# A diffusion block with a gated recurrence on one core: a recurrence with fewer arrays, its gates on quarters of the array, squares moved between engines

## The chip, the cores and the metric

The kernel runs on one core of a Trainium2 chip. The core has a matrix engine (TensorE, PE in the profile), a vector engine (VectorE, DVE), an engine for activation functions (ScalarE, ACT), a general engine (GpSimd, POOL) and a queue engine that issues most transfers (SyncE, SP). The metric is the device time of one execution in microseconds, as the median of several runs.

## The reference, cut to what matters

A token of the 2048 x 1024 input is normalised and modulated, projected to 1536 columns, mixed over time in three branches, projected back, and passed through a convolutional FFN. The change touches the branch with the gated recurrence, and small parts of the others:

```python
r = sigmoid(block_diag(xh, w_a) + b_a)          # 8 heads of 64 x 64, two directions
i = sigmoid(block_diag(xh, w_x) + b_x)
log_a = -8 * r * softplus(-lam)
a = exp(log_a)
bterm = sqrt(-expm1(2 * log_a)) * (i * xf)
h[t] = a[t] * h[t-1] + bterm[t]                 # forward, and backward from the other end
...
ya = gelu(z[..., 512:1024]) * (h_f + h_b)       # gates
yb = pool_group(...)                            # window means of width 2, 4, 8, 16
yc = gmlp_group(...)                            # gelu, norm, 128 x 128 mixing over tokens
mix = concat([ya, yb, yc]) @ w_out
```

The context of 256 tokens runs through the same recurrence first, and its last states start those of the 2048 tokens.

## The kernel before, in words

Activations lie with channels on the 128 partitions and tokens along the row, in four chunks of 512 tokens (`CH`). Weights and activations are split into a high and a low fp16 part, and each product is three matmuls (`mm3`, L356), so that a block of 128 output channels by 512 tokens is 24 matmuls of 512 columns. The mixer fills the first 553 us. It is written as a list of steps (`ORDER`, L37): `x` loads and normalises a chunk, `c` runs the recurrence of the context, `a` projects and convolves a chunk of the recurrent branch, `f` and `b` are a chunk's forward and backward recurrence, `g` is half a step of gMLP, `p` a chunk of pooling, `G` the gates, `m` the modulation vectors, `w` the preparation of the output weights. `P` and `Q` are channel tiles 0, 1 and 2, 3. The list gives priorities; a scheduler places the instructions from it, and each engine then runs its own queue in order, with semaphores between the engines.

A unit of the recurrence is one channel tile and one direction in one chunk; two go together (a pair, `lru_units`, L506). `coeffs` (L440) multiplies the block-diagonal 128 x 128 gate matrices `gwt` in fp32 into two PSUM banks, `rp` and `ip`, and takes two sigmoids and a tanh on ACT. `coeffs2` takes exp on ACT, then r x r and i x xa on POOL and (r x r + 1) x tanh on DVE (`combine`, L459). `coeffs3` takes the square root on ACT and the product i x root on POOL; then DVE scans over time (`scan`, L475). A unit has a buffer of four arrays r, i, t, q of 512 columns, and there are two buffers (`lru_tile`, L176). The forward result goes to DRAM (`hfd`); the backward one is added to it (`join`, L520). Functions of ACT come in table sets, and `act` (L133) keeps instructions of one set together; sigmoid and tanh, exp, the root, and gelu are four sets, each with a table load.

Squares with a sum along the row, from which scales are computed, are taken on ACT (`sumsq`, L149) or on DVE (`vsumsq`, L152): on DVE those of the gated product (`gates`, L640), of the pooling result (`pool_br`, L539) and of the output weights (`wout_stats`, L684). After the mixer, `fold` (L284) joins the FFN's modulation with its gains; `project` then multiplies tokens by the output weights, and the FFN follows.

Of the kernel before, what the change touches and what calls it, by code (L numbers as in the profile page):

```python
# [41 lines left out]
m6 w2 b0P G1Q m6 w2 b0Q G0P m9 G0Q w9 w9  # L42
# [26 lines left out]
def block_kernel(ctx: ExitStack, tc: tile.TileContext, x, xT, ctx_d, ctxT, cc, crow, cols_d, wm01, bm01, wmT,  # L69
# [127 lines left out]
    brow = lru_tile([2, 2048], F32, "brow")  # L197
    lx = load_x(0)
    r23 = lru_tile([128, 2, 1024], F32, "r23")
# [22 lines left out]
    def stats_first(xt):  # L222
        acc = early.tile([128, CH], F32, tag="acc", name="acc")
# [164 lines left out]
    def lam_consts():  # L388
# [21 lines left out]
        V.tensor_scalar(klam, p, -8.0, None, op0=OP.mult)  # L410

# [27 lines left out]

    def coeffs(j, d, xa, w, c=None, bank=None):  # L440
# [12 lines left out]
    def coeffs2(cs, xas, w):  # L453
        for c in cs:
            act(c[0][:, :w], c[0][:, :w], AF.Exp, scale=c[4])
        for c, xa in zip(cs, xas):
            combine(c, xa, w)

    def combine(c, xa, w):  # L459
        r, i, t, q, k = c  # L460
        G.tensor_tensor(q[:, :w], r[:, :w], r[:, :w], op=OP.mult)
        G.tensor_tensor(i[:, :w], i[:, :w], xa, op=OP.mult)
        V.scalar_tensor_tensor(t[:, :w], q[:, :w], 1.0, t[:, :w], op0=OP.add, op1=OP.mult)

    def coeffs3(cs, w):
        for c in cs:
            act(c[2][:, :w], c[2][:, :w], AF.Sqrt, scale=-1.0)
        for c in cs:
            finish_b(c, w)

    def finish_b(c, w):
        i, t = c[1], c[2]
        G.tensor_tensor(i[:, :w], i[:, :w], t[:, :w], op=OP.mult)

    def scan(o, c, w, init, rev):  # L475
        r, i = c[0][:, :w], c[1][:, :w]
# [15 lines left out]
    def lru_ctx(js):  # L492
        jd = [(j, d) for j in js for d in range(2)]
        ts = [lru_tile([128, 4, CH], F32, "lrc") for j in js]
        cs = [coeffs(j, d, xac[0][:, j, :], LC, ts[j - js[0]][:, :, d * LC:(d + 1) * LC]) for j, d in jd]
        coeffs2(cs, [xac[0][:, j, :] for j, d in jd], LC)
        coeffs3(cs, LC)
        for (j, d), c in zip(jd, cs):
            q = c[3]
# [6 lines left out]
    def lru_units(d, n, js, sink):  # L506
        cs = [coeffs(j, d, Y[n][:, j, :], CH, bank=b) for j, b in zip(js, (pB, pA))]
        coeffs2(cs, [Y[n][:, j, :] for j in js], CH)
        coeffs3(cs, CH)
        for j, c in zip(js, cs):  # L510
            o = c[3]
# [86 lines left out]
    def gmlp():  # L598
        ws = wslot["uv"]
        for tp in range(8):  # L600
# [33 lines left out]
            yc = mix.tile([128, 2, 256], F32, tag="yc", bufs=1, name="yc")  # L634
            A.activation(yc, tp_ps.rearrange("p (c t) -> p c t", c=2), AF.Identity)
            sumsq(guv[0].rearrange("p (c t) -> p c t", c=2), yc, ysq[:, n, 6 + r:7 + r])
# [3 lines left out]
    def gates(n, js):  # L640
        for j in js:
            if True:
                ps = pA(f"gt{j}")
                mm_in(ps, 4 + j, n * CH, CH)
                g = late.tile([128, CH], F32, tag="gg", bufs=3, name="gg")
# [588 lines left out]
```

## Time and profile before

| | |
|---|---|
| median of three runs | 2155.48 us (2154.54 to 2159.58) |
| the profiled execution | 2155.6 us, span 2153.8 us |
| PE busy | 2022.0 us, 94% of the span |
| DVE busy | 1593.2 us, 74% |
| ACT busy | 1194.6 us, 55% |
| POOL busy | 610.1 us, 28% |
| mean granted clock of PE | 0.972 |

The table says how busy each engine is over everything. It does not say which engine is last in a stage. For that, the rows further down cut the span into stretches: 148 to 345 us is the forward recurrence beside convolution and gMLP, 345 to 553 us the backward recurrence beside pooling and gates, and from 553 us the output projection starts; the FFN runs at an even pace from about 860 to 2060 us.

### The profile page before, as it was taken

The page shows a single profiled execution, that of the slowest core. Times are in us where ns is not written, and L with a number is a line of the kernel's source. Part 1 is how long each engine was busy: PE and PEld are TensorE (multiplying, and loading weights), DVE is VectorE, ACT ScalarE, POOL GpSimd, SP SyncE. Part 2 cuts the span into 40 slices and gives each one's busy share as a digit, 9 for nine tenths or more (in the row PEclk, how much of TensorE's full clock was granted, in tenths as well). Part 3 has the DMA queues.
Part 4 walks back from the last instruction along what each step waited for, and adds up shares of the span by engine and source line. Part 5 has one row for each costly group of instructions (what it writes and reads, how often), then busy time and mean ns, then how long its engine had stood idle before and what let it go on. Part 6 is the DMA issues. An engine that isn't in the chain of part 4 may idle for free.

```text
span 2153.8 us, 24277 instructions
## 1 busy us (share of the span) xinstructions
PE 2022.0 (94%) x9215; PEld 933.4 (43%) x9215; DVE 1593.2 (74%) x2214; ACT 1194.6 (55%) x1665; POOL 610.1 (28%) x457
## 2 busy tenths in 40 slices
PE   6878989788899998999999999999999999999995
PEld 1433444333455443444444444444444444444442
DVE  5687788999655359978667776867777686777876
ACT  4676756455254555656565554655556465555453
POOL 1233334445155510101121121212112121221156
PEclk8889999998999999999999999999999999999998
DMA  7521152512433210315455454544545454454248
GB/s 297 183 88 74 69 166 89 180 35 85 135 136 114 79 64 20 130 66 132 89 117 98 79 124 72 108 78 102 94 88 100 74 103 88 100 95 69 40 157 156
DMA packets 73480, 224.78 MB, mean 104 GB/s; under 512 B 7442, under 2 KB 18066, under 8 KB 68498
## 3 DMA queue, kind: packets, MB, share of 16 engines
q0 software_dynamic: 21312, 77.60, 21.4%
q1 hardware_dynamic: 52052, 145.64, 19.6%
q8 instruction: 72, 1.18, 0.2%
q14 instruction: 44, 0.36, 0.1%
HBM read 120.45 MB, written 102.76 MB: 104 GB/s over the span
## 4 chain that ended last, share of the span: by engine, by line
PE 55%; DVE 3%; POOL 1%; DMA 1%; ACT 1%; issue 1%; POOLq 0%; SPq 0%; DVEq 0%; ACTq 0%
PE up L359 12%; PE up L360 12%; PE up L361 12%; PE dn L1054 6%; PE dn L1056 6%; PE dn L1055 6%; DVE cv L1011 2%; DMA hT<-accd 1%; POOL hT L1069 0%; DVE hT L1086 0%; DVE hT L1060 0%; DMA wm<-in_wmT_dram 0%; POOL fms L159 0%; PE sct L121 0%; POOL out_dram L1087 0%
## 5 line engine op out<-in xcount | busy, mean ns | idle before, releaser
L1011 DVE SCALAR_TENSOR_TENSOR cv<-z,cols,cv 128x1008 f32<-128x1008 f32 (+3 forms) x704 | 870.4, 1250 | 276.6 <-ACT cv L1005 188.7
L359 PE MATMUL up<-hT,uw 128*128 128x512 f16 x1408 | 534.1, 379 | 2.6 <-ACT z L846 2.6
L361 PE MATMUL up<-hT,uw 128*128 128x512 f16 x1408 | 534.1, 379 | 0.0
L360 PE MATMUL up<-hT,uw 128*128 128x512 f16 x1408 | 534.1, 379 | 0.0
L1071 POOL DMA_DIRECT2D accd<-dd x132 | 114.2, 865 | 704.1 <-ACT dd L1065 697.9
L846 ACT ACTIVATE z<-up,upinv 128x512 f32<-128x512 f32 x176 | 120.5, 685 | 311.2 <-PE up L361 310.8
L1065 ACT ACTIVATE dd<-dn,gdi 128x512 f32<-128x512 f32 x320 | 214.2, 680 | 115.0 <-PE dn L1056 107.5
L1054 PE MATMUL dn<-dw,gs 128*128 128x512 f16 x704 | 267.2, 380 | 7.1 <-ACT dd L1065 5.3
L1055 PE MATMUL dn<-dw,gs 128*128 128x512 f16 x704 | 267.5, 380 | 0.0
L1056 PE MATMUL dn<-dw,gs 128*128 128x512 f16 x704 | 265.8, 380 | 0.0
L360 PEld LDWEIGHTS <-uw 128*128 128x128 f16 x1408 | 137.8, 98 | 167.5 <-issue 3.6
L359 PEld LDWEIGHTS <-uw 128*128 128x128 f16 x1408 | 139.0, 99 | 164.7 <-issue 0.6
L361 PEld LDWEIGHTS <-uw 128*128 128x128 f16 x1408 | 137.8, 98 | 166.5 <-issue 0.6
L832 POOL TENSOR_TENSOR uw<-ur,uw 128x2048 f16<-128x2048 f32 x22 | 89.5, 4070 | 168.9 <-ACT ur L831 168.9
L135 ACT ACT_TABLE_LOAD x77 | 98.8, 1283 | 47.4 <-PE rp L443 28.8
L1005 ACT ACTIVATE cv<-z,cols 128x1024 f32<-128x1024 f32 x88 | 106.0, 1206 | 2.0
L1055 PEld LDWEIGHTS <-gs 128*128 128x128 f16 x704 | 68.8, 98 | 86.8 <-issue 9.5
L1054 PEld LDWEIGHTS <-gs 128*128 128x128 f16 x704 | 72.2, 103 | 78.8 <-issue 0.8
L1056 PEld LDWEIGHTS <-gs 128*128 128x128 f16 x704 | 68.9, 98 | 83.5 <-issue 0.6
L986 POOL TENSOR_TENSOR dw<-dr,dw 128x1024 f16<-128x1024 f32 x22 | 46.4, 2127 | 141.8 <-PE dn L1056 100.3
L150 ACT ACTIVATE junk<-g 128x1024 bf16<-128x1024 f32 x44 | 46.3, 1053 | 59.9 <-DVE g L1019 59.9
L878 PE MATMUL wo<-wo,ysp 128*128 128x512 f16 x256 | 77.1, 383 | 1.0 <-ACT gm L807 1.0
(302 smaller groups left out, 3076.7 us busy)
## 6 DMA issues: line engine op xcount, KB each, us to landing
accd<-dd POOLq DMA_DIRECT2D x132, 512.0 KB, 5.1
ur<-in_wup_dram SPq DMA_DIRECT2D x22, 1024.0 KB, 5.6
wm<-in_wmT_dram SPq DMA_DIRECT2D x64, 256.0 KB, 2.9
dr<-in_wdn_dram SPq DMA_DIRECT2D x22, 512.0 KB, 4.6
hT<-in_wm_dram SPq DMA_DIRECT2D x8, 1024.0 KB, 14.4
xt<-in_xT_dram SPq DMA_DIRECT2D x8, 1024.0 KB, 7.1
ro<-in_wout_dram SPq DMA_DIRECT2D x16, 512.0 KB, 3.8
xr<-in_x_dram SPq DMA_DIRECT2D x16, 512.0 KB, 3.6
```

What stands on the lines that cost most here:

```text
L135: ins = A.activation(out_, in_, func, **kw).ins
L359: T.matmul(ps, wh(k), hh(k), start=(k == 0), stop=False)
L360: T.matmul(ps, wh(k), hl(k), start=False, stop=False)
L361: T.matmul(ps, wl(k), hh(k), start=False, stop=(k == KT - 1))
L846: A.activation(z[:, ab, b * 8:(b + 1) * 8, :], ps.rearrange("p (r x) -> p r x", x=64), AF.Identity, scale=upinv[:, c:c + 1])
L1005: A.activation(t, z[:, ab, r0:r0 + 16, :].rearrange("p r x -> p (r x)"), AF.Identity, bias=col("fcb", c + NP * ab), scale=wt(0, 0))
L1011: V.scalar_tensor_tensor(o, z[:, ab, ya + dy:yb + dy, xa + dx:xb + dx], wt(dy, dx), o, op0=OP.mult, op1=OP.add)
L1054: T.matmul(ps[h], hi, wh, start=i == 0, stop=False)
L1055: T.matmul(ps[h], hi, wl, start=False, stop=False)
L1056: T.matmul(ps[h], lo, wh, start=False, stop=i == n - 1)
L1065: A.activation(d[:, h * CH:(h + 1) * CH], ps[h], AF.Copy, scale=di)
L1071: G.dma_start(accd[t], d, accum_op=OP.add)
```

## The change

- The root: with t = tanh(log a / 2), 1 - a^2 is -t (1 + a)^2, where before it was -tanh(log a)(1 + a^2). The tanh takes half the factor (a new column of constants, -4 softplus, in the place of `lam`), the root is taken of -t directly, and (1 + a) is multiplied into i x xa. POOL's r x r and the array q go; the scan writes into t.
- A unit has three arrays, and there are four buffers instead of two, in a pool of their own. A pool `lru0` holds what shared those buffers in the first 90 us.
- The gates are 64 x 64 matmuls on quarters of the array: for each half of the channels one for `rp` and one for `ip`. The result of `ip` lands with its halves exchanged, and its sigmoid is two instructions of 64 partitions. `gwt` is loaded without its zero blocks, by eight loads.
- The squares in `gates`, `pool_br` and `wout_stats` are taken on ACT.
- `yc` lies in the gMLP's own tile, `acc` in a tile of the squares, and there are two `gg` buffers instead of three.
- `fold` of the FFN is a step of the list (`F`) ahead of the last two backward pairs.

```diff
-m6 w2 b0P G1Q m6 w2 b0Q G0P m9 G0Q w9 w9
+w2 F b0P G1Q w2 b0Q G0P G0Q w9 w9
...
-    gwt = mix.tile([128, 4, 4, 128], F32, name="gwt")
-
-    def lru_tile(shape, dt, name):
-        return mix.tile(shape, dt, tag="lru", bufs=2, name=name)
+    gwt = mix.tile([128, 4, 4, 64], F32, name="gwt")
+    HALVES = (slice(0, 64), slice(64, 128))
...
+        V.tensor_scalar(lam, p, -4.0, None, op0=OP.mult)
...
-        T.matmul(rp[:, :w], gwt[:, j, 2 * d, :], xa, start=True, stop=True)
-        T.matmul(ip[:, :w], gwt[:, j, 2 * d + 1, :], xa, start=True, stop=True)
-        c = lru_tile([128, 4, CH], F32, "lru") if c is None else c
-        r, i, t, q = (c[:, a, :] for a in range(4))
-        act(r[:, :w], rp[:, :w], AF.Sigmoid, bias=col("ba", 4 * d + j))
-        act(i[:, :w], ip[:, :w], AF.Sigmoid, bias=col("bx", 4 * d + j))
-        k = klam[:, 4 * d + j:4 * d + j + 1]
-        act(t[:, :w], r[:, :w], AF.Tanh, scale=k)
-        return r, i, t, q, k
...
+        for h, o in zip(HALVES, HALVES[::-1]):
+            T.matmul(rp[h, :w], gwt[h, j, 2 * d, :], xa[h], start=True, stop=True)
+            T.matmul(ip[o, :w], gwt[h, j, 2 * d + 1, :], xa[h], start=True, stop=True)
+        c = lru_tile("lru") if c is None else c
+        r, i, t = (c[:, a, :w] for a in range(3))
+        act(r, rp[:, :w], AF.Sigmoid, bias=col("ba", 4 * d + j))
+        for h, o in zip(HALVES, HALVES[::-1]):
+            act(i[h], ip[o, :w], AF.Sigmoid, bias=col("bx", 4 * d + j)[h])
+        act(t, r, AF.Tanh, scale=col("lam", 4 * d + j))
+        return r, i, t, klam[:, 4 * d + j:4 * d + j + 1]
+
+    def coeffs2(cs, xas):
+        for r, i, t, k in cs:
+            act(r, r, AF.Exp, scale=k)
+        for r, i, t, k in cs:
+            act(t, t, AF.Sqrt, scale=-1.0)
+        for (r, i, t, k), xa in zip(cs, xas):
+            G.tensor_tensor(i, i, xa, op=OP.mult)
+            V.scalar_tensor_tensor(i, r, 1.0, i, op0=OP.add, op1=OP.mult)
+            G.tensor_tensor(i, i, t, op=OP.mult)
...
-                    vsumsq(a[:, 0:CH], yb[n - 1], ysq[:, n - 1, 4 + pt:5 + pt])
+                    sumsq(a[:, 0:CH], yb[n - 1], ysq[:, n - 1, 4 + pt:5 + pt])
...
-                vsumsq(g, Y[n][:, j, :], ysq[:, n, j:j + 1])
+                sumsq(g, Y[n][:, j, :], ysq[:, n, j:j + 1])
...
-            vsumsq(r, r, t[:, k:k + 1])
+            sumsq(r, r, t[:, k:k + 1])
...
-    S.dma_start(gwt, gw.rearrange("j p g c -> p j g c"))
+    for j in range(4):
+        for h in HALVES:
+            S.dma_start(gwt[h, j], gw[j, h, :, h])
...
+    lruc = tc.tile_pool(name="lru", bufs=4, side="right")
```

The order of instructions shows three places. The first is PE, where the gates of a forward pair of chunk 1 follow a gMLP block (`rp` and `ip` are the two gate banks, `Y1_94` is the chunk's convolved input, `uv` a block of the gMLP; the numbers tell buffers and allocations apart); before:

```order
L361 MATMUL uv_1520<-wsu3_666,hT_82 128x512
L443 MATMUL rp_1556<-Y1_94,gwt_101 128x512
L444 MATMUL ip_1557<-Y1_94,gwt_101 128x512
L443 MATMUL rp_1564<-Y1_94,gwt_101 128x512
L444 MATMUL ip_1565<-Y1_94,gwt_101 128x512
```

and after, the same pair:

```order
L451 MATMUL rp_1597<-Y1_94,gwt_101 64x512
L452 MATMUL ip_1598<-Y1_94,gwt_101 64x512
L451 MATMUL rp_1597<-Y1_94,gwt_101 64x512
L452 MATMUL ip_1598<-Y1_94,gwt_101 64x512
L451 MATMUL rp_1608<-Y1_94,gwt_101 64x512
L452 MATMUL ip_1609<-Y1_94,gwt_101 64x512
L451 MATMUL rp_1608<-Y1_94,gwt_101 64x512
L452 MATMUL ip_1609<-Y1_94,gwt_101 64x512
```

Four matmuls of 128 rows have become eight of 64, and `rp` and `ip` still take turns. The second place is ACT in the backward stretch, one pair with the gates after it (`gt` is the gate projection in PSUM, `gg` its gelu, `klam` and `cols` constants); before:

```order
L135 ACT_TABLE_LOAD
L135 ACTIVATE lru<-rp,cols 128x512
L135 ACTIVATE lru<-lru,klam 128x512
L135 ACTIVATE lru<-ip,cols 128x512
L135 ACTIVATE lru<-rp,cols 128x512
L135 ACTIVATE lru<-ip,cols 128x512
L135 ACTIVATE lru<-lru,klam 128x512
L135 ACT_TABLE_LOAD
L135 ACTIVATE lru<-lru,klam 128x512 x2
L135 ACT_TABLE_LOAD
L135 ACTIVATE lru<-lru 128x512 x2
L135 ACT_TABLE_LOAD
```

and after, from the second tanh of a pair on (`ysq` collects the sums of squares, `yb` is a chunk of the pooling result):

```order
L135 ACTIVATE lru<-ip,cols 64x512 x2
L135 ACTIVATE lru<-lru,cols 128x512
L135 ACT_TABLE_LOAD
L135 ACTIVATE lru<-lru,klam 128x512 x2
L135 ACT_TABLE_LOAD
L135 ACTIVATE lru<-lru 128x512 x2
L135 ACT_TABLE_LOAD
L135 ACTIVATE gg<-gt_3192,inv 128x512
L150 ACTIVATE gg,ysq<-Y_92 128x512
L135 ACTIVATE gg<-gt_3221,inv 128x512
L150 ACTIVATE gg,ysq<-Y_92 128x512
L150 ACTIVATE pa,ysq<-yb 128x512
```

The sets and their loads stay as they were; the sigmoids of `ip` have doubled, and three squares stand behind the gelus. The third place is POOL in the same stretch, two backward pairs of chunk 2 (`hf` is the forward result read back); before:

```order
L462 TENSOR_TENSOR lru_2739<-lru_2739,Y23_92 128x512
L462 TENSOR_TENSOR lru_2747<-lru_2747,Y23_92 128x512
L461 TENSOR_TENSOR lru_2739<-lru_2739 128x512
L461 TENSOR_TENSOR lru_2747<-lru_2747 128x512
L473 TENSOR_TENSOR lru_2739<-lru_2739 128x512
L473 TENSOR_TENSOR lru_2747<-lru_2747 128x512
L523 TENSOR_TENSOR Y23_92<-lru_2739,hf_2765 128x512
L523 TENSOR_TENSOR Y23_92<-lru_2747,hf_2770 128x512
L462 TENSOR_TENSOR lru_2921<-lru_2921,Y23_92 128x512
```

and after:

```order
L467 TENSOR_TENSOR lru_2800<-lru_2800,Y23_92 128x512
L467 TENSOR_TENSOR lru_2811<-lru_2811,Y23_92 128x512
L469 TENSOR_TENSOR lru_2800<-lru_2800 128x512
L469 TENSOR_TENSOR lru_2811<-lru_2811 128x512
L517 TENSOR_TENSOR Y23_92<-lru_2800,hf_2828 128x512
L517 TENSOR_TENSOR Y23_92<-lru_2811,hf_2833 128x512
L467 TENSOR_TENSOR lru_2986<-lru_2986,Y23_92 128x512
```

Two of eight instructions of a pair are gone; the next pair's first product still stands behind the sum with the forward result.

## Rows read from the trace of the kernel before

**Rows 1.** Windows: stretch, length, busy us (instructions) of each engine, granted clock, DMA share, GB/s.

```profile
148.00:345.00 197.00, 177.44 (x745) 82.17 (x745) 154.58 (x318) 137.79 (x188) 71.44 (x64) 0.96 0.26 89
345.00:553.00 208.00, 169.99 (x667) 75.98 (x665) 195.43 (x330) 100.04 (x129) 91.25 (x62) 0.91 0.33 104
...
860.00:2060.00 1200.00, 1196.01 (x5600) 549.62 (x5599) 900.47 (x950) 677.36 (x844) 229.07 (x170) 1.00 0.46 94
```

**Rows 2.** Waits, 345 to 553 us, ACT then PE: us in total, times, longest.

```profile
ACT lru L135 <- DVE lru L463: 31.7, 11, 7.0
ACT L135 <- PE rp L443: 27.8, 4, 9.3
ACT gg L135 <- PE gt L361: 17.6, 6, 4.5
ACT L135 <- DVE state L514: 12.7, 2, 10.2
...
PE pp L535 <- DVE pb L574: 23.1, 6, 6.6
PE sct L121 <- DVE gsfmm L297: 4.6, 1, 4.6
```

**Rows 3.** Waits, 148 to 345 us, DVE.

```profile
DVE lru L463 <- POOL lru L461: 22.7, 5, 7.3
```

**Rows 4.** DVE, lines 479 and 153: count, ns min/median/max, first and last start.

```profile
L479 DVE TENSOR_TENSOR_SCAN lru<-lru,state x32: 1251/1274/2287, 163.8 to 535.6; 128x512 f32<-128x512 f32 x32
...
L153 DVE SCALAR_TENSOR_TENSOR gg<-Y x16: 659/679/1793, 399.0 to 551.0; 128x512 f32<-128x512 f32 x16
L153 DVE DVE_READ_ACCUMULATOR gg<-Y x16: 75/76/84, 399.6 to 551.7; 128x1 f32 x16
L153 DVE SCALAR_TENSOR_TENSOR ro<-ro x8: 1194/1664/2297, 374.8 to 406.8; 128x1024 f32<-128x1024 f32 x8
```

**Rows 5.** Line 153 in a window; line 479 by form (busy us, mean ns), 345 to 553.

```profile
345.00:553.00 208.00, 35.79 (x64) 0.91 0.33 104
...
L479 DVE TENSOR_TENSOR_SCAN lru<-lru,state 128x512 f32<-128x512 f32 x16 | 26.4, 1650 | 2.0 <-POOL lru L473 2.0
```

**Rows 6.** Timeline, DVE then POOL: start us, us, engine, line, operation.

```profile
463.44 0.69 DVE L562 TENSOR_TENSOR pa<-pb 128x521 f32<-128x521 f32 x1
...
464.75 1.66 DVE L562 TENSOR_TENSOR pb<-pa 64x513 f32<-64x513 f32 x1
...
464.32 3.22 POOL L473 TENSOR_TENSOR lru<-lru 128x512 f32<-128x512 f32 x2 [1.35 <-ACT lru L135]
```

**Rows 7.** ACT's squares by form, 148 to 345 us: count, busy us, mean ns, idle.

```profile
L150 ACT ACTIVATE ws<-rw 128x1024 bf16<-128x1024 f32 x6 | 6.3, 1052 | 5.5 <-DMA rw<-in_win_dram 5.5
L150 ACT ACTIVATE guv<-yc 128x512 f32<-128x512 f32 x5 | 3.1, 627 | 0.1
...
L150 ACT ACTIVATION_READ_ACCUMULATOR guv<-yc 128x1 f32 x5 | 0.9, 186 | 0.0
```

**Rows 8.** POOL's r x r by form, 345 to 553 us.

```profile
L461 POOL TENSOR_TENSOR lru<-lru 128x512 f32<-128x512 f32 x16 | 19.7, 1248 | 5.8 <-ACT lru L135 5.8
```

**Rows 9.** Timeline of ACT: two sigmoids of a pair.

```profile
456.38 0.67 ACT L135 ACTIVATE lru<-ip,cols 128x512 f32<-128x512 f32 x1
456.95 0.68 ACT L135 ACTIVATE lru<-rp,cols 128x512 f32<-128x512 f32 x1
```

**Rows 10.** Timeline of PE: the gates of a pair between fp16 blocks.

```profile
474.05 0.38 PE L360 MATMUL pl<-hT,ws 128*128 128x512 f16 x1
474.26 0.38 PE L361 MATMUL pl<-hT,ws 128*128 128x512 f16 x1
474.48 1.02 PE L443 MATMUL rp<-Y,gwt 128*128 128x512 f32 x2
...
477.91 0.38 PE L359 MATMUL gt<-hT,ws 128*128 128x512 f16 x1
```

**Rows 11.** Timeline of SP's queue: the load of the gate matrices.

```profile
22.67 0.39 SPq L718 DMA_DIRECT2D gwt<-in_gw_dram  x1
```

More of the change, by code (lines that the diff above doesn't have):

```diff
@@ L173, in block_kernel @@
     mix = mixc.__enter__()
-    gwt = mix.tile([128, 4, 4, 128], F32, name="gwt")
-    def lru_tile(shape, dt, name):
-        return mix.tile(shape, dt, tag="lru", bufs=2, name=name)
+    gwt = mix.tile([128, 4, 4, 64], F32, name="gwt")
+    HALVES = (slice(0, 64), slice(64, 128))
+    lru0c = tc.tile_pool(name="lru0", bufs=1, side="right")
+    lru0 = lru0c.__enter__()
     earlyc = tc.tile_pool(name="early", bufs=1)
@@ L196, in block_kernel @@
     wmv = hT.bitcast(F32).rearrange("p a k t -> p (a k t)").rearrange("p (k t) -> p k t", k=KT)
-    brow = lru_tile([2, 2048], F32, "brow")
+    brow = lru0.tile([2, 2048], F32, name="brow")
     lx = load_x(0)
-    r23 = lru_tile([128, 2, 1024], F32, "r23")
+    r23 = lru0.tile([128, 2, 1024], F32, name="r23")
     win_raw = [rawt(f"rw{j}") if j < 2 else r23[:, j - 2, :] for j in range(4)]
@@ L222, in stats_first @@
     def stats_first(xt):
-        acc = early.tile([128, CH], F32, tag="acc", name="acc")
+        acc = early.tile([128, 2, CH], F32, tag="xs", bufs=2, name="acc")[:, 0, :]
         sq = early.tile([128, 2, CH], F32, tag="xs", bufs=2, name="sq")
@@ L438, in block_kernel, with lru_tile @@
     state = const.tile([128, 4, 2], F32, name="state")
+    def lru_tile(name):
+        return lrup.tile([128, 3, CH], F32, tag="lru", name=name)
     def coeffs(j, d, xa, w, c=None, bank=None):
@@ L450, in coeffs @@
-        act(t[:, :w], r[:, :w], AF.Tanh, scale=k)
-        return r, i, t, q, k
[L453 to L463, printed above, removed]
@@ L493, in lru_ctx @@
         jd = [(j, d) for j in js for d in range(2)]
-        ts = [lru_tile([128, 4, CH], F32, "lrc") for j in js]
+        ts = [lru_tile("lrc") for j in js]
         cs = [coeffs(j, d, xac[0][:, j, :], LC, ts[j - js[0]][:, :, d * LC:(d + 1) * LC]) for j, d in jd]
-        coeffs2(cs, [xac[0][:, j, :] for j, d in jd], LC)
-        coeffs3(cs, LC)
+        coeffs2(cs, [xac[0][:, j, :] for j, d in jd])
         for (j, d), c in zip(jd, cs):
-            q = c[3]
+            q = c[2]
             scan(q, c, LC, 0.0, d == 1)
@@ L507, in lru_units @@
         cs = [coeffs(j, d, Y[n][:, j, :], CH, bank=b) for j, b in zip(js, (pB, pA))]
-        coeffs2(cs, [Y[n][:, j, :] for j in js], CH)
-        coeffs3(cs, CH)
+        coeffs2(cs, [Y[n][:, j, :] for j in js])
         for j, c in zip(js, cs):
-            o = c[3]
+            o = c[2]
             scan(o, c, CH, state[:, j, d:d + 1], d == 1)
@@ L633, in gmlp @@
                                 v[:, ct * 128:(ct + 1) * 128], ident)
-            yc = mix.tile([128, 2, 256], F32, tag="yc", bufs=1, name="yc")
+            yc = guvt[:, :, 0:256]
             A.activation(yc, tp_ps.rearrange("p (c t) -> p c t", c=2), AF.Identity)
-            sumsq(guv[0].rearrange("p (c t) -> p c t", c=2), yc, ysq[:, n, 6 + r:7 + r])
+            sumsq(guvt[:, :, 256:512], yc, ysq[:, n, 6 + r:7 + r])
             S.dma_start(ybc[n][:, 2:4, r * 256:(r + 1) * 256], yc)
@@ L644, in gates @@
                 mm_in(ps, 4 + j, n * CH, CH)
-                g = late.tile([128, CH], F32, tag="gg", bufs=3, name="gg")
+                g = late.tile([128, CH], F32, tag="gg", bufs=2, name="gg")
                 act(g, ps, AF.Gelu_apprx_tanh, scale=inv[:, 4 + j:5 + j])
                 V.tensor_tensor(Y[n][:, j, :], g, Y[n][:, j, :], op=OP.mult)
-                vsumsq(g, Y[n][:, j, :], ysq[:, n, j:j + 1])
+                sumsq(g, Y[n][:, j, :], ysq[:, n, j:j + 1])
     mcol = const.tile([128, 2, 32], F32, name="mcol")
@@ L753, in late_open, with fold_ffn @@
         S.dma_start(pwt, pw)
-    late = latec = pwt = None
+    late = latec = pwt = gs_f = sc_f = None
+    def fold_ffn():
+        nonlocal gs_f, sc_f
+        gs_f, sc_f, _ = fold("gsf", col("gpf", 0, 8), mcol[:, 0, 8:16], mcol[:, 0, 16:24])
     def prep_ins(*js):
@@ L837, in block_kernel @@
     gm2 = row_of("gm2", on_, 0, col("gqm", 0, 8))
-    gs_f, sc_f, _ = fold("gsf", col("gpf", 0, 8), mcol[:, 0, 8:16], mcol[:, 0, 16:24])
     def up(c, z, w, order=(0, 1, 2, 3)):
```

16 lines of the change are left out of this document (6 added, 10 removed).

## The prediction

> **What bounds the kernel now.** I read the busy time by stage first, because the share over the whole span hides that the stages have different limits [rows 1]. From the first projection at 553 us on, TensorE (PE) is all but full; in the FFN it is busy for 1196.0 of 1200 us. The order of instructions on every engine behind the first projection is the same in both kernels (one small VectorE pair apart), so that nothing before 553 us can shorten what follows it; a microsecond won in the mixer moves the end by a microsecond. The change therefore lives in 553 us, and there the limits differ. In 345 to 553 us, where the backward recurrence, the gates and the pooling branch run, VectorE (DVE) is busy for 195.4 of 208 us, PE for 170.0, ScalarE (ACT) for 100.0 [rows 1]. The waits of that stretch agree: PE waits 23.1 us in front of the pooling matmul for DVE, ACT waits 31.7 us at the root for DVE's product, 27.8 us for `rp` and 12.7 us for a recurrence buffer that DVE still reads [rows 2]. DVE is last. In 148 to 345 us (forward recurrence, convolution, gMLP) PE leads with 177.4 of 197 us and DVE follows with 154.6; DVE idles there for 22.7 us at the combine, waiting for GpSimd's (POOL) square [rows 1, 3].
>
> A second reading matters for the sum. DVE's times contain waits for POOL: a scan is 1.27 us by its median and up to 2.29, a square of `gg` 0.68 and up to 1.79 [rows 4]. The timeline shows why: the 64x513 add takes 1.66 us while POOL runs its product from 464.32, although the larger 128x521 add just before took 0.69 [rows 6]. An instruction of POOL thus costs DVE time as well.
>
> **The change, part by part.** The sum is made against the profiled execution, 2155.6 us (span 2153.8 and 1.8 around it); the median of the runs shown is 2155.48, so nothing has to be corrected.
>
> *Squares to ACT.* 32 squares with their accumulator reads leave DVE, 35.8 us of its busy time in the backward stretch [rows 5]. Not all of it is work: at the shortest durations it is 24 squares of 512 at 0.66 (those of `yb` have the shape of those of `gg`), 8 of 1024 at 1.19 and 32 reads at 0.08, or 28 us; the other 8 us are waits for POOL, and will fall on the neighbouring instruction [rows 4]. ACT pays 24 squares at 0.63 + 0.19 and 8 long ones at 1.05 + 0.19, by its squares of the same shapes: 29.6 us [rows 7].
>
> *Three arrays.* POOL loses r x r: 16 instructions in each of the two stretches (19.7 us backward) and 8 half-size ones before them [rows 8]. What this gives DVE has two bounds per POOL instruction. The scans alone lose 16 x (1.65 - 1.25) = 6.4 us and the squares 8, so the 62 POOL instructions of the stretch cost DVE at least 14 us, 0.23 each [rows 1, 4, 5]; and none can hold it longer than it lasts, 1.25 us here [rows 8]. The add of [rows 6] lost about 1.0. Scans and squares are a third of what can be held, so I take 0.6: sixteen fewer give 10 us back (bounds 4 and 20, and nothing if the next POOL instruction only comes sooner). DVE's backward stretch is then 195.4 - 28 - 10 = 157 us.
>
> *Root from tanh of the half.* The root no longer needs exp, POOL and DVE. ACT's 31.7 us of waiting for the combine [rows 2] go; the root then follows exp at once. What is late next is POOL's last product and the scan, and those are on DVE's own schedule, so I count no gain beside the stretch's bound. On POOL, i x xa is queued ahead of i x t as before, so pairs still pass through POOL one after the other; four buffers free ACT from its 12.7 us for a buffer, and ACT is not last. SP's queue gets seven more small loads of `gwt`, at 0.39 us each [rows 11], ahead of `wst`, `gnr` and the context rows; the projection of the first chunk covers these, and without that cover the price is 7 x 0.39, 3 us. `acc` sharing a buffer with the squares is over before those loads, and `yc` inside `guv` holds a `guv` tile until its store lands, a few microseconds in which PE has other blocks to run.
>
> *Halved sigmoid.* `ip` now lies with its halves exchanged, so its sigmoid is two instructions of 64 partitions. ACT's sigmoid of 128 partitions holds its queue for about 0.6 us (from 456.38 to 456.95), and I take the same for a half (at best 0.3; no gain, since nothing else gets shorter): 14 more in each long stretch, 9 us, and about 3 us before them [rows 9]. ACT's backward stretch: 100 + 29.6 + 9 = 139 us, under DVE's 157.
>
> *Quarters of the array.* This is the open price; the profile has no matmul on a part of the array. A pair of units now costs PE four fp32 matmuls, 8 passes at 0.43 us, from 474.48 to 477.91: 3.43 us [rows 10]. The change makes them 8 matmuls and 16 passes on 64 x 64. If four matmuls run at once, 16 passes take the time of 4, 1.7 us. If none overlap, 6.9 us. In between: a second pass of a quarter must follow its first, and if passes start in queue order, then only the second pass of one quarter and the first of the next overlap: nine steps, 3.9 us, near today's price. The rows lie nearest to this, since the pair's starts stand in the queue's order, two passes of one matmul behind each other; I take it as neutral (+0.4 x 16, half of it hidden: +3).
>
> The Trainium skill, page "TensorE: Matmul & The Clock Gate", part 3 on packing small matmuls, says that matmuls of different tiles overlap but start and end strictly in program order; by that the pair would be the 3.9 us just named. Its page "TensorEngine Tiling (Array Packing)", "Key Properties", adds that a switch of the tiling mode drains the array, which speaks against this change with two switches per pair; no row here shows such a drain.
>
> *Fold sooner.* At the end of the stretch PE waits 4.6 us at `sct` for the FFN fold's maximum [rows 2]. DVE is busy with weight splits in most of that time, so I take 2 us of it (bounds 0 and 4.6).
>
> **The sum.** Backward, by the code: PE has 23 blocks of 24 fp16 matmuls (16 gate blocks, 7 pooling blocks) at 0.215 (119), seven pairs of units at 3.43 (24), 16 passes of the pooling matrix at 0.43 (7) and some 5 of small ones, 155 us at the full clock, which the trace grants for 0.91 of it; DVE needs 157 [rows 1, 10]. Two engines of equal length that wait for each other do not reach the 94% that DVE alone has now; I take 86%, and 157 us become 183: **25 us less** (at 94% 41, at 80% 12). Forward: PE has 25 blocks (14 of gMLP, 10 of the convolution, 1 of the pooling), 129 us, and nine pairs, 31, with 10 of small ones 170 us of the 197. The combine's wait for POOL is gone there, of which PE can use a third: I take 8 us less, 3 of which the quarters cost back: **5 less**. From 100 to 148 us the half sigmoids of the context eat what POOL gives: **2 less**. End: **2 less**. Together 34: **2122 us** (2155.6 - 34 = 2121.6).
>
> **Rivals.** *Four quarters at once.* PE saves 1.7 us per pair, 27 us in 16 pairs. Forward, where PE leads, 14 of these and the combine's waits come through (17); backward PE is down to 143 and DVE alone is last again: 157 at 88%, 178, 30 less; 3 + 2 elsewhere: 52 less, 2104 us. For it: the halves are exchanged so that the quarters of one column half write to different banks. Against: the two passes of each matmul stand next to each other in the queue [rows 10].
>
> The Trainium skill's "TensorEngine Tiling (Array Packing)", "Key Properties", says that tiles work independently and can load and multiply in parallel; by that rule this rival's 2104 holds.
>
> *ACT's order becomes the bound.* The square of Y stands in ACT's queue between two gelus, or ahead of the next pair's sigmoids, and waits for DVE's product: behind it every sigmoid, exp and root is held, and PE's banks with them. ACT's 139 us are 67% of the stretch; with 24 such waits of 1.5 us and today's 17.6 us for `gt` it is 193 of 208: backward 15 less rather than 25, 2132 us.
>
> *The other side: passes that run one after the other.* Then a pair takes 6.9 us. Forward PE needs 170 + 31 = 201 us, at 94% 214, 17 more; backward 155 + 24 = 179, at 93% 193, 15 less; the context's passes double, 5 more, end 2 less; and each of 32 switches of shape shows the tail of the pass before it, 0.16 us (two passes last 1.02 where the next starts after 0.86 [rows 10]), 5 more: +10, 2166 us. Between 3.9 us (34 less) and 6.9 us (10 more) the sign turns at about 6.2 us per pair. For it: no row shows two matmuls streaming at a time. A change that leaves the pair order as it is, so that the four buffers do nothing, is already in my sum.
>
> **How the numbers follow.** About 0.3% (6.5 us) is what a measurement of this kernel can tell from no change. Forecast (neutral quarters, DVE relieved) 0.42, between 2112 and 2134; four at once 0.25; ACT's order 0.15, with a tenth of it within 6 us of today; one after the other 0.18, of which 0.08 ends slower, 0.05 within and 0.05 faster. Faster: 0.42 + 0.25 + 0.13 + 0.05 = 0.85, which I take as 0.82 for what no case names; within 0.09; slower 0.09. Range 2094 to 2160 us: it takes in the forecast, ACT's case, all but the lower tail of four at once and the middle of the serial case; about 0.17 is left out.
>
> **What would show it.** In the profile after: `L150` on DVE gone and ACT longer by some 30 us backward; POOL's r x r gone, and DVE's scan mean in the backward stretch under 1.6 us. PE's wait at `pp` for DVE should fall under 12 us. The two stretches should end near 340 and 519 us. The quarters: eight matmul starts per pair within 1.7, 3.9 or 6.9 us decide between the forecast and two rivals. ACT's waits for `Y` and `gg` above 30 us would show the third. The prediction is wrong if the FFN's 1200 us change at all, or if the backward stretch stays above 200 us although DVE's busy time fell.

## The result and the profile after

The changed kernel takes 2177.89 us (median of 4 runs, 2176.9 to 2179.18) against 2155.01 us before: a ratio of 1.0104, with an interval of 1.0086 to 1.0122. It is 22 us slower where 33 us less were forecast, and lies above the range. The profiled execution took 2179.2 us, its span is 2177.4.

By the end of the last scan the loss is there: before, the last scan of the recurrence ended at 537.9 us and the first projection began at 553.05 us; after, these are 560.7 and 580.68. Behind the projection 4 us come back, where the forecast had nothing move; what gave them was not followed. The FFN did not change, as the third row shows beside its counterpart of [rows 1]. Windows of the changed kernel (stretch, length, busy us and instructions of PE, PE's weight loads, DVE, ACT and POOL, granted clock, DMA share, GB/s):

```profile
148.00:345.00 197.00, 165.95 (x776) 71.22 (x776) 135.08 (x304) 140.39 (x189) 47.70 (x41) 0.89 0.26 87
345.00:553.00 208.00, 162.25 (x732) 68.50 (x732) 134.57 (x265) 143.62 (x215) 66.27 (x49) 0.90 0.30 98
...
887.00:2087.00 1200.00, 1197.26 (x5613) 550.64 (x5612) 903.22 (x954) 678.74 (x846) 229.06 (x170) 1.00 0.46 95
```

In the same windows of time as [rows 1], DVE's busy time is 61 us less in the second, POOL's 25, PE's 8, and ACT's 44 more. But the changed kernel's stretch ends 28 us later, so that some of its work lies behind the window. The stretch from the end of the eighth pair's last scan to the first projection holds about the same work in both; first before, then after:

```profile
337.10:553.05 215.95, 177.89 (x703) 79.99 (x702) 202.02 (x346) 107.90 (x140) 95.62 (x67) 0.91 0.32 101
350.60:580.68 230.08, 168.37 (x768) 72.58 (x769) 149.90 (x293) 149.76 (x225) 68.46 (x51) 0.88 0.32 103
```

By these DVE lost 52 us, POOL 27 and PE 10, ACT gained 42, and the stretch is 14 us longer: the sign that the prediction named for being wrong, a backward stretch above 200 us although DVE's busy time fell. No engine is busy for more than 85% of a window now. The relieved engines wait. Waits of the changed kernel from 345 to 553 us, DVE, ACT and PE (us in total, times, longest), beside [rows 2, 3]:

```profile
DVE lru L468 <- ACT lru L135: 36.5, 7, 8.1
DVE wm L654 <- DMA wm<-in_wmT_dram: 10.4, 5, 3.8
...
ACT gg L150 <- DVE Y L641: 27.7, 11, 5.9
ACT ro L150 <- DMA ro<-in_wout_dram: 15.2, 3, 12.8
ACT pa L150 <- DVE yb L531: 8.8, 4, 4.2
...
PE pp L529 <- DVE pb L568: 19.9, 4, 6.7
PE pp L529 <- DVE pb L574: 8.4, 2, 6.6
```

DVE now stands at the combine until ACT's exp is through, 36.5 us here and 66.3 from 148 to 553 us; before it stood there for POOL's square, 25.1 us. ACT in turn stands at the moved squares until DVE's product is there. Its 143.6 busy us and some 60 us of waiting fill the 208. PE's wait at `pp` for DVE, which was to fall under 12 us, is 28.3 in its two largest rows (19.9 + 8.4), in place of 27.1 (23.1 + 4.0).

The quarters of the array work as the most hopeful rival had it. Timeline of PE around a pair's gates (start us, us, engine, line, operation), beside [rows 10]:

```profile
189.31 0.38 PE L362 MATMUL xa<-hT,ws 128*128 128x512 f16 x1
189.62 0.64 PE L451 MATMUL rp<-Y,gwt 64*64 64x512 f32 x1
189.62 0.64 PE L452 MATMUL ip<-Y,gwt 64*64 64x512 f32 x1
189.63 0.64 PE L451 MATMUL rp<-Y,gwt 64*64 64x512 f32 x1
189.63 0.64 PE L452 MATMUL ip<-Y,gwt 64*64 64x512 f32 x1
190.09 0.59 PE L451 MATMUL rp<-Y,gwt 64*64 64x512 f32 x1
...
190.97 0.59 PE L452 MATMUL ip<-Y,gwt 64*64 64x512 f32 x1
191.50 0.39 PE L360 MATMUL uv<-wsu,hT 128*128 128x512 f16 x1
```

Four passes start within 0.01 to 0.03 us, and the 16 passes take 189.62 to 191.50, 1.88 us instead of 3.43. PE is ahead by 1.55 us per pair, and the kernel is slower.

### The profile page after: what moved, and what is told of

Same layout as the page of the kernel before. It is cut to its first block, busy times and chain, and to the rows that moved or that the text cites. A ratio compares the mean times of both kernels' runs of the same rounds, so it can differ in the third digit from the quotient of the medians.

```text
span 2177.4 us, 24599 instructions
## 1 busy us (share of the span) xinstructions
PE 2007.4 (92%) x9375; PEld 913.4 (42%) x9375; DVE 1521.2 (70%) x2151; ACT 1250.1 (57%) x1769; POOL 560.4 (26%) x417
## 4 chain that ended last, share of the span: by engine, by line
PE 55%; DVE 3%; POOL 1%; issue 1%; DMA 1%; ACT 1%; SPq 0%; POOLq 0%; DVEq 0%; ACTq 0%
PE up L360 12%; PE up L361 12%; PE up L362 12%; PE dn L1058 6%; PE dn L1060 6%; PE dn L1059 6%; DVE cv L1015 2%; POOL hT L1073 0%; DVE hT L1090 0%; DMA hT<-accd 0%; DVE hT L1064 0%; DMA wm<-in_wmT_dram 0%; POOL fms L159 0%; PE sct L121 0%; POOL out_dram L1091 0%
```

## The experiments

Ratios are to the kernel before, measured beside it; us are the ratio applied to 2155.

| kernel | ratio (interval) | us |
|---|---|---|
| changed | 1.0104 (1.0086 to 1.0122) | +22 |
| e1_hold | 1.0101 (1.0082 to 1.0119) | +22 |
| e2_dve_squares | 1.0112 (1.0091 to 1.0133) | +24 |
| e3_one_sigmoid | 1.0048 (1.0033 to 1.0063) | +10 |
| e4_old_root | 1.0094 (1.0078 to 1.0110) | +20 |
| e5_three_buffers | 1.0116 (1.0099 to 1.0133) | +25 |
| e6_own_yc | 1.0082 (1.0065 to 1.0100) | +18 |
| e7_quarters_alone | 1.0063 (1.0043 to 1.0083) | +14 |
| e8_root_alone | 0.9988 (0.9975 to 1.0000) | -3 |
| e9_quarters_one_sigmoid | 0.9985 (0.9975 to 0.9994) | -3 |
| e10_half_sigmoids | 1.0044 (1.0029 to 1.0059) | +9 |
| e11_act_squares_alone | 0.9984 (0.9974 to 0.9993) | -3 |
| e12_all_but_two | 0.9972 (0.9961 to 0.9982) | -6 |
| e13_squares_cut | 0.9989 (0.9980 to 0.9999) | -2 |
| e14_no_ip_sigmoid | 0.9990 (0.9978 to 1.0002) | -2 |
| e15_fold_late | 0.9965 (0.9953 to 0.9976) | -8 |
| e16_best_hold | 0.9959 (0.9943 to 0.9974) | -9 |
| e17_half_in_context | 0.9972 (0.9957 to 0.9987) | -6 |
| e18_half_in_long | 1.0039 (1.0024 to 1.0054) | +8 |

**Undoing one part of the changed kernel.** At the end of the mixer ACT's first square of an FFN weight block stands ahead of the last two gelus, and waits 5.3 us for its load; PE waits 15.4 us at `sct`. The first run holds that square back:

```diff
-            stat(w[0].bitcast(BF16), [r], upsc[:, c, :])
+            stat(w[0].bitcast(BF16), [r], upsc[:, c, :], gate_sq[-1:] if c == 0 else ())
...
```

> The changed kernel with one order added: the square of the FFN's first weight block (uw) stands on ACT behind the last square of the gates, instead of two gelus earlier. In the trace of the changed kernel that square waits 5.3 us for its load, which itself waits until the last recurrence buffer is read, and PE idles 15.4 us at sct behind it. Theory A (the end of the mixer is a real loss of this order): the wait at sct falls to about 6 us, the first projection comes at about 572 us, total 2178 - 8 = 2170. Rival (the loss is before the end, and what stands behind the end takes up whatever is won there): 2178 within 2.

The wait at `sct` is still 13.3 us, and the total moved by less than a microsecond. The square was in the way; what is left of the wait is behind other late work, by the trace of this run DVE's `yt`. The next run moves the squares back:

```diff
...
-                sumsq(g, Y[n][:, j, :], ysq[:, n, j:j + 1])
+                vsumsq(g, Y[n][:, j, :], ysq[:, n, j:j + 1])
...
-            sumsq(r, r, t[:, k:k + 1])
+            vsumsq(r, r, t[:, k:k + 1])
```

> The changed kernel with the squares of the gated product, of the pooling result and of the output weights back on VectorE. Theory A (ACT's queue is what holds the backward stretch: 144 us busy and 64 us of waiting, of which 29 for Y, 9 for yb, 15 for the weights' load, all at the moved squares): ACT loses 30 us of work and those waits, VectorE gets 28 us into its 70 us of idle time: backward stretch 20 us shorter, total 2158. Rival B (the loss lies in the order and the buffers, not in ACT's load): VectorE is longer again, nothing is won, 2178 to 2190. Rival C (PE's quarters bring the clock down): as B.

Nothing was won: rival B. Whichever engine has the squares, the changed kernel takes the same time. The third run puts both gates of a half on one quarter, so that one sigmoid does:

```diff
-            T.matmul(ip[o, :w], gwt[h, j, 2 * d + 1, :], xa[h], start=True, stop=True)
+            T.matmul(ip[h, :w], gwt[h, j, 2 * d + 1, :], xa[h], start=True, stop=True)
...
-        for h, o in zip(HALVES, HALVES[::-1]):
-            act(i[h], ip[o, :w], AF.Sigmoid, bias=col("bx", 4 * d + j)[h])
+        act(i, ip[:, :w], AF.Sigmoid, bias=col("bx", 4 * d + j))
```

> The changed kernel with both gates of a half on the same quarter of the array, so that the result of ip lies in its own place and one sigmoid of 128 partitions reads it. With the weights of two different gates on one quarter, two matmuls can run at once, not four: a pair should take some 3.5 us on PE instead of 1.9, 27 us more PE time in 16 pairs. ACT loses 0.8 us per unit (1.38 us for the two halves against 0.57), 26 us in 32 units. Theory A (ACT's queue holds): half of the 26 us comes through, 2165. Rival B (order and buffers): 2178 within 4. Rival C (PE counts): 2190.

Half of the loss went, 12 us, and it went although PE's pair takes 3.63 us again (185.68 to 189.31 in its trace). PE's mean granted clock is 0.972 as before the change; in the changed kernel it is 0.961. But the trace puts the gain at the first pair: its last scan ends at 164.4 us, in the changed kernel at 178.8, and the distance is 10 to 14 us at every later pair and 13.8 at the last. Timeline of ACT there, the changed kernel (eight normalisations of a chunk ahead of the pair's first sigmoid) and then e3_one_sigmoid:

```profile
149.06 5.33 ACT L262 ACTIVATE hT<-xt,gsl 128x512 f16<-128x512 f32 x8 [0.21 <-DVE xt L261]
...
158.56 0.69 ACT L135 ACTIVATE lru<-rp,cols 128x512 f32<-128x512 f32 x1
```

```profile
142.21 0.69 ACT L135 ACTIVATE lru<-rp,cols 128x512 f32<-128x512 f32 x1
...
146.55 3.36 ACT L262 ACTIVATE hT<-xt,gsl 128x512 f16<-128x512 f32 x5 [1.23 <-DVE xt L261]
```

ACT's queue has another order there. This run therefore doesn't tell the price of the instructions from that of the order, and no run holds the order fixed. The old root (four arrays, three buffers) was next:

> The changed kernel with the old root: tanh of the whole, r x r on POOL, (r x r + 1) x tanh on VectorE, then the root; four arrays and three buffers, everything else as changed. Theory A (ACT's queue holds): ACT waits again at the root for VectorE's product, some 20 to 40 us in all, POOL does 32 more products: 2185 to 2200. Rival B (the new order of the recurrence, with the combine waiting on exp in VectorE's queue for 66 us, is what lost): 2165 or less.

It changes 2 us, neither theory's number: the root is not where the time went. Then the buffers and `yc`:

```diff
...
-    lruc = tc.tile_pool(name="lru", bufs=4, side="right")
+    lruc = tc.tile_pool(name="lru", bufs=3, side="right")
...
```

> The changed kernel with three recurrence buffers instead of four, and the tiles that use that space in the first 90 us sharing two places again; yc still in the gMLP's tile. It is the control for the next run. Theory A (the fourth buffer does nothing, since each pair is through before the one after next begins): 2178 within 4. Rival B (the buffers matter, pairs overlap): 2185 or more.

```diff
-            yc = guvt[:, :, 0:256]
+            yc = mix.tile([128, 2, 256], F32, tag="yc", bufs=1, name="yc")
...
```

(With three buffers, what uses their space in the first 90 us shares two places again, in both runs.)

> As e5_three_buffers, and yc in a tile of its own as before the change. In the trace of the changed kernel ACT waits 15.2 us, three times, between 310 and 351 us for the store of yc to DRAM: the store stands in SyncE's queue behind loads of modulation weights (wm) that wait for VectorE, and the next gelu needs the same tile. All changed variants so far lose about 12 us between the seventh and the ninth pair (63.8 us there against 51.7 before). Theory A (that wait is this loss): the piece falls to about 52 us, the total by 10 to 12 us against e5_three_buffers, to about 2166. Rival B (the wait is covered, ACT is late anyway): within 4 us of e5_three_buffers.

The fourth buffer does nothing. An own `yc` gives 7 us. Waits of ACT from 300 to 375 us, e5_three_buffers:

```profile
ACT guv L135 <- DMA ybc<-guv: 15.1, 3, 8.3
ACT guv L629 <- PE tp L626: 12.9, 3, 6.2
```

and e6_own_yc:

```profile
ACT yc L629 <- PE tp L626: 11.5, 2, 7.8
ACT guv L135 <- PE uv L362: 10.9, 2, 6.7
```

The wait for the store is gone, and a wait of ACT for PE's next block stands in its place; 7 of 15 us came through. The piece between the seventh and the ninth pair, which was to fall to 52 us, fell from 64.2 to 60.2 only, so the rest of the gain lies elsewhere, and that piece had another cause than I gave it. Why the store is late stands in SyncE's queue of the changed kernel (start us, us, operation):

```profile
309.74 1.83 SPq L512 DMA_DIRECT2D hfd<-lru  x2
312.69 0.32 SPq L516 DMA_DIRECT2D hf<-hfd  x1
313.10 0.86 SPq L653 DMA_DIRECT2D wm<-in_wmT_dram  x2
314.05 0.38 SPq L631 DMA_DIRECT2D ybc<-guv  x1
```

`yc` was written at 309.65 us; its store was issued at 314.05, behind two stores of the recurrence that wait for their scans and the loads of `hf` and `wm`, and the gelu that needs the tile began at 318.95.

**One part alone on the kernel before.** First the quarters with their two half sigmoids, then the new root:

> The kernel before with the gates on quarters of the array alone (half-size weights, eight matmuls per pair, the two half sigmoids), nothing else. A pair takes 1.9 us on PE instead of 3.4 and ACT 1.6 us more. Theory A (ACT's queue is near the path and the half sigmoids cost more than PE wins): 2160 to 2168. Rival B (PE leads in the forward stretch, and its 14 us there come through): 2140. Rival C (the loss is in the order of VectorE's queue at the first pair, which this part sets: 8 us): first pair done near 178 us instead of 171.

> The kernel before with the new root alone (tanh of the half, root after exp, combine on i x xa, no r x r), in buffers of before. VectorE's 25 us of waiting for POOL's square and ACT's 42 us for the combine go; VectorE then waits for exp at the combine. Theory A (it is a shorter chain, and what lost is elsewhere): 2145. Rival B (VectorE stands at the combine until ACT's exp, and its other work behind it: 66 us in the changed kernel): 2155 to 2170.

The quarters alone cost 14 us, the root alone is even. For the quarters, two runs part what PE and what ACT do: four quarters with one sigmoid over `ip` as it lies (which leaves out the exchange of the halves, so that the output is not the reference's), and full gates with two half sigmoids. The second one's edit:

```diff
-        act(i[:, :w], ip[:, :w], AF.Sigmoid, bias=col("bx", 4 * d + j))
+        for h in HALVES:
+            act(i[h, :w], ip[h, :w], AF.Sigmoid, bias=col("bx", 4 * d + j)[h])
```

> The kernel before with the four quarters as in e7_quarters_alone, but with one sigmoid of 128 partitions over ip as it lies, so that the two halves of i are exchanged and the output is not the reference's. It leaves the 0.8 us per unit of the second half sigmoid out and keeps what PE does. Theory A (what the quarters cost is the second sigmoid on ACT): 2150 or less, since PE still wins 1.55 us per pair. Rival B (PE's clock: in the runs with four quarters the mean granted clock is 0.960 to 0.962, with full gates or two at once 0.971 to 0.972): the clock stays at 0.961 and the time near 2167.

> The kernel before with full gates and the sigmoid of ip as two instructions of 64 partitions: only what ACT pays. 0.8 us per unit, 26 us in 32 units. Theory A: most of the 14 us of e7_quarters_alone and perhaps more, since PE wins nothing: 2165 to 2172, granted clock about 0.97 or a little less. Rival B: within 4 us of before, 2153.

Four quarters on PE gain 3 us, the half sigmoids lose 9. The clock of e9_quarters_one_sigmoid is 0.970, so the quarters as such don't lower it. Then the squares:

> The kernel before with the squares of the gated product, of the pooling result and of the output weights on ACT, nothing else. VectorE loses 36 us of 195 in the backward stretch. The forecast counted this as the largest gain, some 15 to 20 us. Theory A (ACT's queue then holds sigmoids behind squares that wait for VectorE, as the 35 us and 9 us of such waits in the changed kernel show): 2148 to 2158. Rival B (VectorE is what is last there): 2138 or less.

They bring 3 us where the forecast had most of its 25. Is that ACT's share taking the gain away? The next run cuts the squares to 64 columns on DVE and gives ACT nothing; the one after it takes one sigmoid per unit away from ACT. Both leave out a part of the computation.

```diff
...
-                vsumsq(g, Y[n][:, j, :], ysq[:, n, j:j + 1])
+                vsumsq(g[:, 0:64], Y[n][:, j, 0:64], ysq[:, n, j:j + 1])
...
```

> The kernel before with the 32 squares of VectorE cut to 64 columns each, so that most of their sums is left out and the output is not the reference's. VectorE loses some 25 to 30 us of 195 in the backward stretch, and ACT gets nothing for it. Theory A (the pass of a pair through ACT, POOL and VectorE sets the pace, not VectorE's sum): within 8 us of before, 2147 to 2154, near e11_act_squares_alone. Rival B (VectorE bounds the stretch, and in e11 ACT took the gain away): 2125 to 2135.

```diff
-        act(i[:, :w], ip[:, :w], AF.Sigmoid, bias=col("bx", 4 * d + j))
...
-        G.tensor_tensor(i[:, :w], i[:, :w], xa, op=OP.mult)
+        G.tensor_tensor(i[:, :w], r[:, :w], xa, op=OP.mult)
```

> The kernel before without the sigmoid of ip: r stands in for i, so one ACT instruction of about 0.6 us per unit is left out and the output is not the reference's. PE still computes ip. Theory A (ACT's pass is on the path in both long stretches: 0.7 us more per unit cost 9.5 us in e10_half_sigmoids): 18 us less of ACT work bring 6 to 10 us, 2145. Rival B (only the extra instruction's order cost, not ACT's time): within 3 us of before.

Neither relief comes through. e13_squares_cut, 345 to 553 us, first the window and then waits of DVE and PE, beside [rows 1, 2]:

```profile
345.00:553.00 208.00, 171.20 (x688) 77.50 (x686) 171.68 (x340) 103.42 (x134) 86.96 (x65) 0.92 0.34 107
...
DVE lru L463 <- POOL lru L461: 14.8, 5, 7.4
DVE wo L312 <- DMA ro<-in_wout_dram: 7.9, 2, 4.2
...
PE sct L121 <- DVE gsfmm L297: 12.8, 1, 12.8
PE pp L535 <- DVE pb L574: 11.7, 5, 4.1
```

DVE has 23.7 us less work than in [rows 1] and waits for POOL and for loads instead, 14.8 us at the combine where it was 2.4. PE's wait at `pp` falls from 23.1 to 11.7 us as forecast, and its wait at `sct` rises from 4.6 to 12.8. The end moved by 2. Part of that is order again: at the ninth pair, before the first cut square, this run is 3.8 us late (360.4 against 356.6), and at the sixteenth 1.4 early, so the relief itself is worth some 5 of 24 us by then.

**Where in the stretch the half sigmoids cost.** e10_half_sigmoids ends its first pair at 179.9 us, 9 later than before, and I took that for the whole price. Two runs tell the context's eight units from the 32 long ones:

> The kernel before with the sigmoid of ip halved in the eight units of the context alone: 8 instructions of 0.47 us more. Theory A (the price is the order and the chain at the context and the first pair): first pair done near 178 us, 2160. Rival B (the price is ACT's time in each long pair): within 3 us of before, first pair near 171.

> The kernel before with the sigmoid of ip halved in the 32 units of the long stretches alone: 32 times 0.7 us more on ACT, 22 us. Theory A (the context's order is the price): 2153 to 2157. Rival B (ACT's time in each pair): 2160 to 2163, spread over the pairs.

The reading fell. With the halves in the context the first pair ends at 178.6 us, 8 late, and the next at 196.8, 3 early; the run is 6 us faster. With the halves in the long units the first pair is on time (171.1), and the delay grows: 3 us by the fifth pair, 7 by the ninth, 10 by the sixteenth. e10_half_sigmoids agrees: its late start is gone by the third pair, which ends at 221.0 us there and at 220.9 in e18_half_in_long (218.7 before), and the two stay within about 1 us of each other to the end. In these two runs the price is paid pair by pair.

**What is left of the change.** e12 undoes the quarters and the shared `yc`; the next two move the fold back and hold the FFN's first square.

> The changed kernel with the two parts undone that have shown a price: gates on the full array with one sigmoid for ip, and yc in a tile of its own (three buffers, for the space). If the prices add (13 for the quarters with their half sigmoids, 8 for yc): 2157. If what is left of the change is worth something once these are gone (squares on ACT, new root, fold sooner): 2145. If something else is still lost at the end of the mixer (13 to 15 us of waiting at sct in all changed variants against 4.6 before): 2160 or more.

> e12_all_but_two with the FFN's fold back at its place behind the mixer. The forecast gave the earlier fold 2 us. Theory A (PE's wait at sct is set by the last gated product and its square, not by the fold): 2149 within 3. Rival B (the earlier fold is worth what it says): 2152 or more.

> e12_all_but_two with the FFN's first square held behind the last square of the gates. There PE waits 14.0 us at sct before the projection. Theory A (that square's wait for its load, 5.6 us, is part of it): 2144 to 2147. Rival B (VectorE's weight splits between the last products are what is late, as e1_hold showed: 13.3 us instead of 15.4): 2147 to 2150.

The rest of the change is 6 us faster than the kernel before, and with the fold at its old place or the square held it is 8 and 9; the three intervals overlap, so these two edits can't be told from nothing. All three versions beat the changed kernel, and the kernel before by 0.3 to 0.4%, which is little more than a change of order gave in e17_half_in_context.

## Why the prediction was wrong

Two steps failed, and e12_all_but_two tells their sizes. Between the forecast's 34 us less and the 22 more lie 56 us. The quarters with their half sigmoids and the shared `yc` cost 28 together (changed against e12) where the sum had 3: 25 us. The rest of the change gained 6 where the sum, without those 3, had 37: 31 us.

**The first step that failed is the one that hides ACT's new work.** The forecast had ACT at 139 us in the backward stretch "under DVE's 157", and therefore charged nothing for the half sigmoids and the squares. The amount there was right: 39 us more were forecast, and 42 measured in the stretch with about the same work. (The price of a half was taken as 0.6 us, and it is 0.8 by 1.38 against 0.57; and the nine forward pairs are 18 more, not 14.) A half sigmoid takes 0.68 us, so that ACT's instructions on `ip` double from 21.7 to 43.2 us in both long stretches of e18_half_in_long:

```profile
L135 ACT ACTIVATE lru<-ip,cols 64x512 f32<-64x512 f32 x64 | 43.2, 675 | 3.0 <-PE ip L445 2.6
```

The cover was not there. A busy share says what an engine has left over a stretch, not what it has left between the gates of a pair and its scan. There DVE's combine stands behind ACT's queue. Timeline of ACT through one pair, changed kernel:

```profile
227.56 1.28 ACT L135 ACT_TABLE_LOAD   x1 [0.38 <-PE ip L452]
228.86 0.69 ACT L135 ACTIVATE lru<-rp,cols 128x512 f32<-128x512 f32 x1
229.58 0.72 ACT L135 ACTIVATE lru<-lru,cols 128x512 f32<-128x512 f32 x1
230.31 1.38 ACT L135 ACTIVATE lru<-ip,cols 64x512 f32<-64x512 f32 x2
231.71 0.69 ACT L135 ACTIVATE lru<-rp,cols 128x512 f32<-128x512 f32 x1
232.43 1.38 ACT L135 ACTIVATE lru<-ip,cols 64x512 f32<-64x512 f32 x2
233.83 0.72 ACT L135 ACTIVATE lru<-lru,cols 128x512 f32<-128x512 f32 x1
234.57 1.28 ACT L135 ACT_TABLE_LOAD   x1
235.86 1.33 ACT L135 ACTIVATE lru<-lru,klam 128x512 f32<-128x512 f32 x2
```

From the table load to the start of exp are 8.30 us; in e12_all_but_two, with one sigmoid for `ip`, the same pass goes from 232.02 to 238.41, 6.39 us, so it is 1.9 us shorter. DVE's wait at the combine of this pair, in the changed kernel and then in e12_all_but_two:

```profile
236.68 1.30 DVE L468 SCALAR_TENSOR_TENSOR lru<-lru 128x512 f32<-128x512 f32 x2 [6.51 <-ACT lru L135]
```

```profile
239.23 1.31 DVE L466 SCALAR_TENSOR_TENSOR lru<-lru 128x512 f32<-128x512 f32 x2 [5.01 <-ACT lru L135]
```

Of the 1.9 us, 1.5 appear there, in the one pair that was followed. Over the kernel a third comes through: e18_half_in_long has 0.8 us more per unit in ACT's queue, 25.6 us in 32 units, and is 8 us slower.

**The second, and the larger: DVE was read as the bound, and is not.** The sum took 195 of 208 busy us and the 23 us of PE's waiting at `pp` for proof that relief of DVE shortens the backward stretch. The four single reliefs say otherwise: DVE by 24 us (e13) 2 us, ACT by 18 (e14) 2, PE by 25 (e9, 16 pairs at 1.55) 3, POOL with the new root (e8) 3. These figures are net of what another order did: the four runs end their first pair at 172.6, 165.9, 175.7 and 166.0 us (170.6 before), and from the first pair to the sixteenth they take 363.9, 374.9, 361.3 and 369.4 (367.3 before). Small they are by either count. I read it as engines that hold each other in a ring of in-order queues, with no one of them last throughout; the waits of e13, where a relieved engine waits at the next hand-over, fit that, and no run shows the ring itself. The right size for the backward term was 3 us by e11, at most some 6 to 9 by e12, e15 and e16, not 25. The Trainium skill's page "Perfetto Trace Analysis", "Identifying the Most-Contended Engine", says to find the engine with the highest occupancy and to optimise it first. For this stretch e13 disagrees: the engine at 94% gave 2 us for 24.

**The quarters.** Of the three prices for a pair, 1.7, 3.9 and 6.9 us, I chose the wrong one; it is 1.88. The nine-step case rested on the two passes of a matmul standing next to each other; the rows of after alternate between `L451` and `L452` within 0.02 us, so they do not. The Trainium skill's page "TensorE: Matmul & The Clock Gate", Part 3, has tiles start in program order some 4 ns apart. The rows agree with that order, in steps of up to 10 ns; I had read the order as a hindrance, which only adjacent passes would have made it. Its page "TensorEngine Tiling (Array Packing)", "Key Properties", says that a switch of the mode drains the array. The rows show about 0.1 us on either side (from 189.31 + 0.215 to 189.62 on the way in), where [rows 10] have no gap. But the sign of this part does not hang on PE: the two half sigmoids belong to it, and the sum put them at nothing. With them the quarters alone lose 14 us, without them they gain 3. The loss is 7 us more than e9 and e10 add up to (9.5 - 3.2 = 6.3, against 13.6). PE's granted clock from 148 to 345 us is 0.89 in e7_quarters_alone and 0.95 in e9; whether that is cause or consequence of longer waits of PE stays open.

**`yc` in the gMLP's tile** was put at "a few microseconds in which PE has other blocks to run". It measured 7 us (e5 against e6). The step named the store as short, 2 us from issue to landing, and did not ask what stands ahead of it in SyncE's queue.

**The moved fold** was to give 2 us and gave none (e12 against e15). **The root and the three arrays** were to take 10 us of contention off DVE. The combine fell from 942 ns in the mean to 690, but the scans, forecast under 1.6 us, rose from 1650 ns [rows 5] to 1794:

```profile
L475 DVE TENSOR_TENSOR_SCAN lru<-lru,state 128x512 f32<-128x512 f32 x16 | 28.7, 1794 | 6.6 <-POOL lru L469 6.6
L468 DVE SCALAR_TENSOR_TENSOR lru<-lru 128x512 f32<-128x512 f32 x16 | 10.6, 690 | 37.0 <-ACT lru L135 36.5 <-issue 0.5
```

POOL's square was not what the scan collides with. The scans of 2.2 to 2.3 us stand beside POOL's last product for the second unit (434.49 us, with the product from 433.18 to 435.68) or beside its sum with the forward result (491.37, with the sum from 490.93), and both stay.

**The rival "ACT's order becomes the bound"** named the mechanism, down to the squares that wait between two gelus, and still came out at 2132: it counted ACT's waits at 36 + 18 us against a stretch that was shortened by DVE's relief, when the relief itself was not there to be had. Its sign, waits for `Y` and `gg` above 30 us, came out at 27.7 for `Y`, and 36.5 with the square of `yb`. The forecast's right points are small: the FFN's 1200 us did not move, ACT rose by some 40 us, and the fourth buffer did nothing visible; after the eight small loads the context's gates start at 90.78 us where it was 90.79.

What stays open: small differences. In e17_half_in_context eight instructions more on ACT made the kernel 6 us faster. The extra instructions do no work that could help; but the scheduler placed parts of DVE's, PE's and ACT's queues in another order. A difference of up to 6 us between two versions whose order moved may therefore be the order's. That holds for the 2 to 3 us of e8, e9, e11, e13 and e14, for which only "small" is shown, and in part for the 7 us of `yc`, where the vanished wait stands beside the number. The 8 to 14 us of e7, e10 and e18 all point one way and exceed it, but 6 us is one case and no bound; the 12 us of e3 lie where the order changed.

## What to carry to other kernels

Where several engines hand one piece of work round through in-order queues, a busy share of 94% is no proof of a bound: before counting a relief, follow one piece through all queues, and look for the wait that takes the place of the one removed. An instruction that is added between the first and the last hand-over of such a pass is not hidden by the free time of its engine; here a third of it was paid. A list scheduler that gets other instructions makes other queues, so a part's price needs the trace, pair by pair, and not only the end. A part of a change that frees one engine and loads another has one price, and it is the sum's sign that counts: here 25 us won on PE were worth 3, and 26 us spent on ACT cost 9.

## What the runs showed of the hardware

An activation on 64 partitions of 512 columns takes as long as one on 128: two halves hold ACT's queue for 1.38 us, two full ones in a row start 0.57 us apart. Four 64 x 64 fp32 matmuls on different quarters stream at once (1.88 us for 16 passes, 3.43 us for 8 passes on the full array), two gates on the same two quarters only two at a time (3.63 us). PE's mean granted clock was 0.961 in the changed kernel, 0.970 with the same quarters and one sigmoid, and 0.972 before; the shape of the matmuls alone does not lower it.
